# SwiGLU with 22 feature tiles: twenty of them in pairs, and an output projection whose last two tiles come late

## The chip, the cores and the metric

The kernel runs on one core of a Trainium2 chip. The metric is the device time of one execution in microseconds (us); of several runs the median is given. Engines are named as in the profile: PE is TensorE (matmul), PEld its weight load, DVE VectorE, ACT ScalarE, POOL GpSimd, SP SyncE, which issues the DMA transfers here. A line such as L503 is a line of the kernel's source.

## The reference

Four decoder layers, each a token mixer (another kind in each layer) and a SwiGLU channel mixer. Both are wrapped in a modulation by a condition vector and a layer norm. There are 512 tokens of width 1024, all in float32. What matters here is the channel mixer and its frame; its hidden width is 2816.

```python
def swiglu(h, w_in, w_out):
    gu = h @ w_in
    return (jax.nn.silu(gu[..., :FFN_HIDDEN]) * gu[..., FFN_HIDDEN:]) @ w_out

# in reference(), the second half of each layer
h = x * (1 + scale[1][:, None]) + shift[1][:, None]
y = swiglu(h, ffn_w_in[i], ffn_w_out[i])
x = layer_norm(DEEPNORM_ALPHA * x + (1 + gate[1][:, None]) * y.astype(x.dtype), ln_g[i, 1], ln_b[i, 1])
```

## The kernel before

**Tiles.** The hidden width is cut into 22 feature tiles of 128. Everything is held with features on the partitions and the 512 tokens along the free axis. A float32 matmul is made of three matmuls in a reduced type: each operand is split into a high part (a copy on ACT, `wh` for weights) and a low part (a subtraction on DVE, `wl`), and high x high, high x low, low x high are summed (`mm3`, L204 to L206). A weight tile of 128 x 1024 comes by one DMA into a buffer called `raw`, issued by SP.

**A plain tile** needs its gate and its up projection: each 8 steps along the width of 1024, 3 matmuls in each, 512 columns, so 48 matmuls. Then come silu on ACT, the product with the up projection on DVE, and its split in a copy on ACT and a subtraction on DVE (`gated` in `ffn`, L575 to L578), into a tile called `pair`.

**A pair of tiles** is one 2 x 2 block product in Strassen's way (`strassen`): seven products of 24 matmuls of 256 columns instead of eight. They are made in the order 1, 2, 6, 5, 7, 4, 3 of the code. Its weights come as four tiles R0 to R3 by DMA (L495); DVE adds and subtracts some of them (L517, L543), and each product needs one split (L480 on ACT, L481 on DVE). Products 1, 6 and 7 are copied out of their accumulation bank by ACT (L514). The two halves of the tokens are finished apart (gating L555, copy L556, subtraction L557).
The inputs of products 4 to 7 are sums of the input's blocks, made once per layer by `t_forms` (L471 on ACT, L472 on DVE) from four buffers H. These H buffers are taken from the same seven `raw` buffers as the weight tiles, so that four weight tiles can only be loaded once the forms are made.

**The order in a layer.** Tiles 0 and 1 come first (`proj_cols` with "t": all tokens' first half, then the second), then tile 2, then nine pairs (tiles 3 to 20). Tile 21 is a plain tile too; its gate and up projections (`last(0)`, `last(1)`) are placed between products of the last pair. The last two products of each pair are placed among the first products of the next pair.

**Output projection.** It is run in three groups of feature tiles, 7, 8 and 7 (`FGROUPS`), each as soon as its tiles are done: for each of eight blocks of 128 output features one weight tile, 3 matmuls of 512 columns for each feature tile of the group, and an addition into the residual `xz` on DVE (L341). In the last group, blocks 4 to 7 are made in two halves of 256 tokens, so that the layer norm of the first half runs beside the second.
Between the weight splits of the output projections the kernel places loads of conditioning weights (`ada_w`), each followed by a reduction on DVE (L128); `self.rate` says how many per weight tile: 2 in the first two groups, 1 in the last. In layer 3 none is left for the last group.

**What sets the order.** The code above is the order in which work is handed to a scheduler, which puts each engine's instructions in a row; each engine works its row off in that order, and waits where an operand isn't there.

## Time and profile before

| | us |
|---|---|
| median of 3 runs | 2435.06 (2433.79 to 2435.41) |
| the profiled execution | 2436.47 |
| its span in the trace | 2434.8 |
| busy: PE | 2378.1 (98%) |
| busy: DVE | 1794.9 (74%) |
| busy: ACT | 1102.6 (45%) |
| busy: POOL | 481.8 (20%) |

The mean granted clock of TensorE over the span is 0.995 of full speed. The span is what the trace covers of the profiled execution; the 1.7 us beside it lie before and after. Matmuls are pipelined, so the duration of one (0.40 us for 512 columns) is longer than the distance from one start to the next; the distances are what counts in a dense stretch. "Idle before" a group of instructions is time in which that engine waited, and the name behind the arrow is what ended the wait.

### The profile page before, as it was taken

What the parts mean: (1) busy time and instruction counts of PE and PEld (TensorE: products, weight loads), DVE (VectorE), ACT (ScalarE), POOL (GpSimd) and SP (SyncE); (2) the same over time, 40 slices, a digit from 0 to 9 for tenths busy, and PEclk for the clock granted to TensorE, in tenths of its full rate; (3) what the DMA queues carried; (4) which work ended last, traced back from release to release, by engine and by line L of the source; (5) the groups of instructions that cost most, each with busy time, mean ns of one, the idle gap of its engine ahead of it and who ended that gap; (6) DMA issues with size and microseconds to landing.
All of it is one profiled execution on the core that took longest, in us unless ns stands there. A gap on an engine that the chain in (4) does not pass through costs nothing.

```text
span 2434.8 us, 40054 instructions
## 1 busy us (share of the span) xinstructions
PE 2378.1 (98%) x15464; PEld 2123.0 (87%) x15464; DVE 1794.9 (74%) x3137; ACT 1102.6 (45%) x1917; POOL 481.8 (20%) x734
## 2 busy tenths in 40 slices
PE   7999999999899999999999999999999999999998
PEld 5778999998668989899888899898988888999897
DVE  6956988886887978787755569788867556968565
ACT  2534644343553635244333336352445554635343
POOL 5003200004434000006433331000053223100003
PEclk9999999999999999999999999999999999999999
DMA  9832363743411363652521113637525111333331
GB/s 317 285 118 87 105 216 95 245 142 121 144 53 53 103 209 114 232 188 85 162 79 61 35 57 117 205 107 236 186 94 173 62 36 44 109 112 101 106 102 35
DMA packets 93999, 312.31 MB, mean 128 GB/s; under 512 B 10736, under 2 KB 13168, under 8 KB 93808
## 3 DMA queue, kind: packets, MB, share of 16 engines
q1 hardware_dynamic: 92800, 309.43, 39.6%
q8 instruction: 121, 1.98, 0.3%
q14 instruction: 70, 0.57, 0.1%
q10 hardware_dynamic: 1008, 0.32, 0.1%
HBM read 307.62 MB, written 2.10 MB: 127 GB/s over the span
## 4 chain that ended last, share of the span: by engine, by line
PE 80%; DVE 9%; ACT 4%; DMA 3%; POOL 3%; issue 2%; POOLq 0%; ACTq 0%; DVEq 0%; SPq 0%
PE ps L503 27%; PE ps L204 14%; PE ps L206 14%; PE ps L205 14%; DVE wl L195 2%; PE ps L1086 1%; DMA raw<-in_ada_w 1%; PE ps L1252 1%; DVE raw L128 1%; ACT wh L194 1%; PE ps L943 1%; DVE xz L412 1%; POOL H L448 1%; DVE xz L420 1%; DVE hl L449 1%
## 5 line engine op out<-in xcount | busy, mean ns | idle before, releaser
L194 ACT ACTIVATE wh<-raw 128x1024 fp32r<-128x1024 f32 (+1 forms) x251 | 257.9, 1031 | 382.9 <-DMA raw<-in_ffn_out 116.1
L480 ACT ACTIVATE wh<-raw 128x1024 fp32r<-128x1024 f32 x252 | 266.1, 1060 | 351.2 <-PE ps L503 134.2
L503 PE MATMUL ps<-tf,wh 128*128 128x256 f32 x2304 | 410.8, 280 | 0.0
L195 DVE TENSOR_TENSOR wl<-raw,wh 128x1024 fp32r<-128x1024 f32 (+1 forms) x251 | 304.3, 1214 | 99.8 <-ACT wh L194 84.2
L481 DVE TENSOR_TENSOR wl<-raw,wh 128x1024 fp32r<-128x1024 f32 x252 | 305.9, 1221 | 80.1 <-ACT wh L480 78.3
L503 PEld LDWEIGHTS ps<-tf,wh 128*128 128x128 f32 x2304 | 353.3, 188 | 0.9
L503 PE MATMUL ps<-tf,wl 128*128 128x256 f32 x1152 | 321.7, 279 | 0.0
L205 PE MATMUL ps<-pair,wh 128*128 128x512 f32 (+1 forms) x816 | 294.4, 361 | 1.5 <-DVE pair L578 1.3
L204 PE MATMUL ps<-pair,wh 128*128 128x512 f32 (+1 forms) x816 | 294.9, 361 | 0.0
L206 PE MATMUL ps<-pair,wl 128*128 128x512 f32 (+1 forms) x816 | 293.9, 360 | 0.0
L128 DVE CUSTOM_DVE_ANT_0 raw<-raw,cond,adab 128x1024 f32<-128x1024 f32 x192 | 246.6, 1294 | 45.3 <-DMA raw<-in_ada_w 43.9
L341 DVE SCALAR_TENSOR_TENSOR xz<-ps,gate,xz 128x512 f32<-128x512 f32 (+1 forms) x208 | 129.8, 625 | 159.7 <-PE ps L206 159.3
L503 PE MATMUL ps<-hh,wl 128*128 128x256 f32 x864 | 245.0, 284 | 0.0
L503 PE MATMUL ps<-hh,wh 128*128 128x256 f32 x864 | 244.7, 283 | 0.0
L503 PE MATMUL ps<-hl,wh 128*128 128x256 f32 x864 | 244.6, 283 | 0.0
L204 PE MATMUL ps<-wh,hh 128*128 128x512 f32 (+1 forms) x608 | 239.3, 395 | 4.6 <-ACT hh L445 3.3
L204 PE MATMUL ps<-hh,wh 128*128 128x256 f32 (+1 forms) x616 | 208.0, 344 | 18.1 <-ACT wh L194 15.6
L206 PE MATMUL ps<-wh,hl 128*128 128x512 f32 (+1 forms) x608 | 222.5, 366 | 0.0
L205 PE MATMUL ps<-wl,hh 128*128 128x512 f32 (+1 forms) x608 | 222.3, 366 | 0.1
L503 PEld LDWEIGHTS ps<-tf,wl 128*128 128x128 f32 x1152 | 216.7, 188 | 0.0
L206 PE MATMUL ps<-hh,wl 128*128 128x256 f32 (+1 forms) x616 | 209.9, 343 | 5.5 <-DVE wl L195 5.5
L205 PE MATMUL ps<-hl,wh 128*128 128x256 f32 (+1 forms) x616 | 207.9, 340 | 0.2
(292 smaller groups left out, 4957.9 us busy)
## 6 DMA issues: line engine op xcount, KB each, us to landing
raw<-in_ada_w SPq DMA_DIRECT2D x192, 512.0 KB, 4.6
raw<-in_ffn_dp SPq DMA_DIRECT2D x144, 512.0 KB, 3.9
raw<-in_ffn_out SPq DMA_DIRECT2D x64, 448.0 KB, 3.6
raw<-in_ffn_in SPq DMA_DIRECT2D x32, 512.0 KB, 3.7
raw<-in_ffn_out SPq DMA_DIRECT2D x32, 512.0 KB, 4.6
raw<-in_m_vo SPq DMA_DIRECT2D x16, 512.0 KB, 5.8
raw<-in_h_qf SPq DMA_DIRECT2D x16, 512.0 KB, 4.1
raw<-in_h_ig SPq DMA_DIRECT2D x16, 512.0 KB, 3.8
```

The source lines that it names most:

```text
L128: self.nc.vector.tensor_tensor_reduce(w, w, self.cond, 1.0, self.adab[:, sub, j : j + 1], ALU.mult, ALU.add, mod[:, j : j + 1])
L194: nc.scalar.activation(hi[:, :n], raw[:, :n], AF.Copy)
L195: (eng or nc.vector).tensor_tensor(lo[:, :n], raw[:, :n], hi[:, :n].bitcast(F32), ALU.subtract)
L204: nc.tensor.matmul(ps, lhs[0], rhs[0], start=start, stop=False)
L205: nc.tensor.matmul(ps, lhs[0], rhs[1], start=False, stop=False)
L206: nc.tensor.matmul(ps, lhs[1], rhs[0], start=False, stop=stop)
L341: nc.vector.scalar_tensor_tensor(z, ps[:, t], gate[:, d : d + 1], z, ALU.mult, ALU.add)
L412: V.tensor_tensor(z, z, st[:, 0, :], ALU.subtract)
L420: V.tensor_tensor(z, z, st[:, 1, :], ALU.mult)
L480: nc.scalar.activation(hi, raw, AF.Copy)
L481: nc.vector.tensor_tensor(lo, raw, hi.bitcast(F32), ALU.subtract)
L503: nc.tensor.matmul(ps[:, j * 256 : j * 256 + 256], w[a][:, c], m[b], start=first and j == k == a == b == 0, stop=k == 3 and a == 1, skip_g ...
```

## The change

Plain are now only tiles 0 and 1 (`FPLAIN`); tiles 2 to 21 go in ten pairs. The groups are 8, 8 and 6 tiles: tiles 0 and 1 with three pairs, four pairs, three pairs. The function `last` is gone. The last group's output projection gets `late=2`: for its first two blocks it first makes the matmuls of the four tiles of the two earlier pairs, for the one block and the other, and then those of the last pair's two tiles. Only then are the two sums added to the residual; blocks 2 to 7 go as before.

```diff
--- before.py
+++ after.py
@@ constants
 DEPTH = 4
 HID = 2816
 KF = HID // P
-FGROUPS = (7, 8, 7)
-FPLAIN = (0, 1, 2, KF - 1)
+FGROUPS = (8, 8, 6)
+FPLAIN = (0, 1)
 ALPHA = (2 * DEPTH) ** 0.25
 LN_EPS = 1e-5
 RMS_EPS = 1e-6
@@ out_proj
                 done(2 * pair + i, pss[i])
-    def out_proj(self, srcs, per, acts, gate, last):
+    def out_proj(self, srcs, per, acts, gate, last, late=0):
         nc = self.nc
         n = len(acts)
-        def mm(ps, w, o, t):
-            for k in range(n):
+        def mm(ps, w, o, t, ks=range(n)):
+            for k in ks:
                 self.mm3(
                     ps[:, t],
                     [x[:, o + k * P : o + (k + 1) * P] for x in w],
...
             (nc.vector if d == KD - 1 else nc.gpsimd).tensor_tensor(s2, s2, sq, ALU.add)
         halves = (4 * per) if last else 0
-        for d0 in range(0, KD - halves, per):
+        if late:
+            ws = [self.weights(srcs[d], n * P) for d in range(2)]
+            pss = [self.bank() for _ in range(2)]
+            for ks in (range(n - late), range(n - late, n)):
+                for d in range(2):
+                    mm(pss[d], ws[d], 0, slice(0, T), ks)
+                    yield 0.65 * len(ks)
+            for d in range(2):
+                fold(pss[d], d, slice(0, T))
+        for d0 in range(2 if late else 0, KD - halves, per):
             w = self.weights(srcs[d0 // per], per * n * P)
             for i in range(per):
                 ps = self.bank()
@@ ffn
             if i == KD - 2:
                 self.pools("ffn")
                 forms = self.t_forms()
-        pa, pb = self.pair_tile(), self.pair_tile()
+        pa = self.pair_tile()
         yield from first
-        yield from self.proj_cols(src(2), None, lambda ps: gated(pb, 0, *ps))
-        acts = [pa[:, :, 0, :], pa[:, :, 1, :], pb[:, :, 0, :]]
+        acts = [pa[:, :, 0, :], pa[:, :, 1, :]]
         n = (KF - len(FPLAIN)) // 2
         ends = np.cumsum(FGROUPS)
         j0 = 0
-        bank = []
-        def last(x):
-            w = self.weights(src(3)[x], D)
-            ps = self.bank()
-            for k in range(KD):
-                self.mm3(
-                    ps,
-                    [y[:, k * P : (k + 1) * P] for y in w],
-                    [self.hh[:, k, :], self.hl[:, k, :]],
-                    k == 0,
-                    k == KD - 1,
-                )
-            bank.append(ps)
         def begin(i):
             act = self.pair_tile()
...
             nxt = begin(i + 1) if i + 1 < n else None
             if nxt:
                 self.advance(nxt[0], 1)
-            else:
-                last(0)
             self.advance(g, 1)
             if nxt:
                 self.advance(nxt[0], 1)
             self.advance(g, 1)
             yield 0.0
             acts += [act[:, :, 0, :], act[:, :, 1, :]]
-            if nxt is None:
-                last(1)
-                pc = self.pair_tile()
-                gated(pc, 0, *bank)
-                acts.append(pc[:, :, 0, :])
             cur, left = nxt, 5
             gn = len(acts)
             if j0 + gn in ends:
@@ where the last output projection is made
                 for x in self.keep.values():
                     self.nc.gpsimd.memset(x[:, 0, 0:1], 0.0)
-            out = self.out_proj(srcs, per, acts, gate, True)
+            out = self.out_proj(srcs, per, acts, gate, True, 2 if kind == "ffn" else 0)
             while next(out) != "A":
                 pass
             ln = self.layer_norm(subs[i], nxt, 0)
@@ host (layout of the weights)
     r["ffn_in"] = w[..., FPLAIN, :].transpose(0, 4, 2, 3, 1, 5).reshape(DEPTH, len(FPLAIN), P, 2, D)
     n = (KF - len(FPLAIN)) // 2
-    w = w[..., 3 : 3 + 2 * n, :].reshape(DEPTH, 2, 4, P, 2, n, 2, P).transpose(0, 5, 4, 1, 3, 6, 2, 7)
+    w = w[..., 2 : 2 + 2 * n, :].reshape(DEPTH, 2, 4, P, 2, n, 2, P).transpose(0, 5, 4, 1, 3, 6, 2, 7)
     w = w.reshape(DEPTH, n, 4, P, D)
     r["ffn_dp"] = w[:, :, [0, 1, 3, 2]]
     w = f("ffn_w_out").reshape(DEPTH, KF, P, KD, P)
```

The start of the first pair, in layer 0. ACT's row after the input forms, before (`b_390` and `b_391` are the silus of tiles 0 and 1, `wh_2425` the high part of tile 2's up projection, `wh_2487` on those of the pair's weights):

```order
L575 ACT_TABLE_LOAD
L575 ACTIVATE b_390_2407<-ps_2112 128x512
L575 ACTIVATE b_391_2412<-ps_2114 128x512
L194 ACTIVATE wh_2425<-raw_2423 128x1024
L577 ACTIVATE pair_2405<-b_390_2407 128x512
L577 ACTIVATE pair_2405<-b_391_2412 128x512
L575 ACTIVATE b_400_2479<-ps_2429 128x512
L480 ACTIVATE wh_2487<-raw_2485 128x1024
L480 ACTIVATE wh_2520<-raw_2518 128x1024
```

and after (`b_396` is the copy of product 1, `wh_2452` the high part of product 2's weights, `wh_2489` of product 6's):

```order
L585 ACT_TABLE_LOAD
L585 ACTIVATE b_389_2406<-ps_2112 128x512
L585 ACTIVATE b_390_2411<-ps_2114 128x512
L524 ACTIVATE b_396_2448<-ps_2423 128x512
L490 ACTIVATE wh_2452<-raw_2450 128x1024
L587 ACTIVATE pair_2405<-b_389_2406 128x512
L587 ACTIVATE pair_2405<-b_390_2411 128x512
L490 ACTIVATE wh_2489<-raw_2417 128x1024
L490 ACTIVATE wh_2519<-raw_2485 128x1024
```

The copy of product 1 now stands ahead of the split of product 2's weights, and both stand ahead of the copies of tiles 0 and 1; the silu and the copy of tile 2 are gone.

DVE's row at the same place, after the subtractions of the input forms, before (`wl_2426` is the low part for tile 2, `wl_2488` and `wl_2521` those of products 1 and 2 of the pair):

```order
L576 TENSOR_TENSOR b_390_2407<-ps_2113,b_390_2407 128x512
L576 TENSOR_TENSOR b_391_2412<-ps_2115,b_391_2412 128x512
L195 TENSOR_TENSOR wl_2426<-raw_2423,wh_2425 128x1024
L578 TENSOR_TENSOR pair_2405<-b_390_2407,pair_2405 128x512
L578 TENSOR_TENSOR pair_2405<-b_391_2412,pair_2405 128x512
L517 TENSOR_TENSOR raw_2553<-raw_2553,raw_2551 128x1024
L481 TENSOR_TENSOR wl_2488<-raw_2485,wh_2487 128x1024
L481 TENSOR_TENSOR wl_2521<-raw_2518,wh_2520 128x1024
L517 TENSOR_TENSOR raw_2485<-raw_2485,raw_2553 128x1024
L576 TENSOR_TENSOR b_400_2479<-ps_2430,b_400_2479 128x512
```

and after (`raw_2417`, `raw_2450`, `raw_2483`, `raw_2485` are R0 to R3, `wl_2453`, `wl_2490`, `wl_2520` the low parts for products 2, 6 and 5):

```order
L527 TENSOR_TENSOR raw_2485<-raw_2485,raw_2483 128x1024
L586 TENSOR_TENSOR b_389_2406<-ps_2113,b_389_2406 128x512
L586 TENSOR_TENSOR b_390_2411<-ps_2115,b_390_2411 128x512
L491 TENSOR_TENSOR wl_2453<-raw_2450,wh_2452 128x1024
L588 TENSOR_TENSOR pair_2405<-b_389_2406,pair_2405 128x512
L588 TENSOR_TENSOR pair_2405<-b_390_2411,pair_2405 128x512
L527 TENSOR_TENSOR raw_2417<-raw_2417,raw_2485 128x1024
L527 TENSOR_TENSOR raw_2450<-raw_2450,raw_2417 128x1024
L527 TENSOR_TENSOR b_396_2448<-ps_2456,b_396_2448 128x512
L491 TENSOR_TENSOR wl_2490<-raw_2417,wh_2489 128x1024
L491 TENSOR_TENSOR wl_2520<-raw_2485,wh_2519 128x1024
```

The add of R3 and R2 has come to the front of the row. The low part of product 2 stands behind the two products of tiles 0 and 1, and that of product 6 behind the addition of products 1 and 2 (`b_396`). The row of product 1's low part is earlier than what is shown.

The end of the last pair in layer 0. DVE's row before (`b_694` and `b_707` are the two halves of the last pair, `b_727` and `pair_5179` the last plain tile, `wl_5266` and on weights of the output projection):

```order
L555 SCALAR_TENSOR_TENSOR b_694_4855<-ps_4830,b_694_4855 128x512
L195 TENSOR_TENSOR wl_5266<-raw_5263,wh_5265 128x896
L557 TENSOR_TENSOR pair_4823<-b_694_4855,pair_4823 128x2x256
L128 ISA raw_5359,mod_2087<-raw_5359,cond,adab 128x1024
L128 ISA mod_2087 128x1
L517 TENSOR_TENSOR b_707_4989<-ps_4995,b_707_4989 128x512
L195 TENSOR_TENSOR wl_5302<-raw_5299,wh_5301 128x896
L555 SCALAR_TENSOR_TENSOR b_707_4989<-b_713_5049,b_707_4989 128x512
L128 ISA raw_5368,mod_2087<-raw_5368,cond,adab 128x1024
L128 ISA mod_2087 128x1
L557 TENSOR_TENSOR pair_4823<-b_707_4989,pair_4823 128x2x256
L576 TENSOR_TENSOR b_727_5180<-ps_5154,b_727_5180 128x512
```

and after (`b_705` and `b_718` are the two halves of the last pair, `pair_4996`; another reduction L128 stands directly ahead of the first row):

```order
L128 ISA raw_5452,mod_2087<-raw_5452,cond,adab 128x1024
L128 ISA mod_2087 128x1
L565 SCALAR_TENSOR_TENSOR b_705_5028<-ps_5003,b_705_5028 128x512
L195 TENSOR_TENSOR wl_5398<-raw_5395,wh_5397 128x768
L567 TENSOR_TENSOR pair_4996<-b_705_5028,pair_4996 128x2x256
L527 TENSOR_TENSOR b_718_5162<-ps_5168,b_718_5162 128x512
L195 TENSOR_TENSOR wl_5431<-raw_5428,wh_5430 128x768
L565 SCALAR_TENSOR_TENSOR b_718_5162<-b_724_5222,b_718_5162 128x512
L128 ISA raw_5461,mod_2087<-raw_5461,cond,adab 128x1024
L128 ISA mod_2087 128x1
L567 TENSOR_TENSOR pair_4996<-b_718_5162,pair_4996 128x2x256
```

Two reductions of conditioning weights (L128) now stand directly ahead of the first half's gating, and a third ahead of the last subtraction; the gating and the subtraction of the plain tile are gone.

## The prediction

> **What bounds the kernel now.** I read the page's busy shares first, then the chain that ended last, then the PE timeline of the SwiGLU of layer 0 (it begins at 271.94 us), and then ACT, DVE and SP at its two ends, where the change moves work.
>
> ```profile
> PE 2378.1 (98%) x15464; PEld 2123.0 (87%) x15464; DVE 1794.9 (74%) x3137; ACT 1102.6 (45%) x1917; POOL 481.8 (20%) x734
> PE 80%; DVE 9%; ACT 4%; DMA 3%; POOL 3%; issue 2%; POOLq 0%; ACTq 0%; DVEq 0%; SPq 0%
> 374.01 79.84 PE ps L503 x672
> ```
>
> PE is busy 98% of the span and holds 80% of the chain. The third row is one link of it: four pairs, 672 matmuls of 256 columns, without a pause. So two things decide: how many matmul columns PE streams, and whether it must wait. The rates come from the timeline (start, duration, engine, line; in brackets a wait and what ended it).
>
> ```profile
> 271.94 0.40 PE L204 MATMUL ps<-hh,wh 128*128 128x512 f32 x1
> 277.98 0.50 PE L204 MATMUL ps<-hh,wh 128*128 128x512 f32 x1 [0.42 <-ACT wh L194]
> 279.24 0.51 PE L206 MATMUL ps<-hh,wl 128*128 128x512 f32 x1 [0.53 <-DVE wl L195]
> 284.40 0.28 PE L503 MATMUL ps<-hh,wh 128*128 128x256 f32 x1
> ...
> 540.00 0.40 PE L204 MATMUL ps<-hh,wh 128*128 128x512 f32 x1
> 545.48 0.40 PE L503 MATMUL ps<-tf,wh 128*128 128x256 f32 x2
> 551.19 0.40 PE L204 MATMUL ps<-hh,wh 128*128 128x512 f32 x1
> 556.66 0.39 PE L204 MATMUL ps<-pair,wh 128*128 128x512 f32 x1
> 562.08 0.50 PE L205 MATMUL ps<-pair,wh 128*128 128x512 f32 x1 [0.43 <-DVE pair L578]
> ```
>
> The first group is the third plain tile, 48 matmuls between tiles 0 and 1 and the first pair. The second holds the last plain tile: gate (540.00 to 545.48), one product of the last pair, then up (551.19 to 556.66), after which the output projection starts. 24 matmuls of 512 columns take 5.48 us, 0.228 each. A pair takes 79.84 / 4 = 19.96 us, 0.119 per matmul of 256 columns.
>
> **The work on PE.** Per layer, two plain tiles become a pair: four projections at 5.48 us leave (-21.9) and a pair comes (+19.96). In the split halves of the last output projection six tiles stand where seven did, so of the same 22 tiles 24 matmuls of 256 columns (2.87 us) become 12 of 512 in another group (2.73): -0.15. The third tile's block also held its own waits: 284.40 - 271.94 = 12.46 us, of which 48 matmuls explain 10.93; the 1.53 left goes too. Sum: -3.6 us a layer.
>
> **The start of the pairs.** In the old order these 12.46 us of the third tile hide what the first pair needs. In the new order PE runs product 1 of the first pair right after tiles 0 and 1 (from 271.94, 24 x 0.119, to 274.8), and then needs product 2's weights split. The engines at that place:
>
> ```profile
> 270.68 3.90 ACT L471 ACTIVATE tf<-H 128x1024 fp32r<-128x1024 f32 x4 [1.47 <-DVE H L464]
> 274.60 1.28 ACT L575 ACT_TABLE_LOAD   x1
> 275.90 1.09 ACT L575 ACTIVATE b<-ps 128x512 f32<-128x512 f32 x2
> 276.87 1.06 ACT L194 ACTIVATE wh<-raw 128x1024 fp32r<-128x1024 f32 x1
> ...
> 271.77 4.63 DVE L472 TENSOR_TENSOR tf<-H,tf 128x1024 fp32r<-128x1024 f32 x4
> 276.53 1.29 DVE L576 TENSOR_TENSOR b<-ps,b 128x512 f32<-128x512 f32 x2
> 277.96 1.23 DVE L195 TENSOR_TENSOR wl<-raw,wh 128x1024 fp32r<-128x1024 f32 x1
> 279.10 1.29 DVE L578 TENSOR_TENSOR pair<-b,pair 128x512 fp32r<-128x512 f32 x2
> 280.31 1.22 DVE L517 TENSOR_TENSOR raw<-raw,raw 128x1024 f32<-128x1024 f32 x1
> ...
> 273.07 2.55 SPq L495 DMA_DIRECT2D raw<-in_ffn_dp  x3
> DMA to landing us min/median/max: 3.6/3.6/3.6
> L514 ACT ACTIVATE b<-ps 128x512 f32<-128x512 f32 x108 | 62.7, 581 | 7.3 <-PE ps L503 7.3
> ```
>
> ACT first makes the four input forms (to 274.6), then loads the table and does two silus (to 277.0). Behind them now stands the copy of product 1 (0.58, the last row), and only then the split of product 2's weights (1.06): high half at about 278.5. DVE has the forms until 276.4. Then, first in its queue, comes an add of two weight tiles (1.13 by its pitch), which waits for a transfer that can be issued only when a form's buffer is free (273.07) and needs 3.6 to land, 276.7: the add ends at 277.9. Two gated products (1.2 together) end at 279.1, then the low half of product 2's weights (1.2) at 280.3. So PE does two matmuls at 278.5 and the rest of product 2 from 280.35, to 283.0. The third product waits again: DVE has two more subtractions of tiles 0 and 1, two weight adds and the add of product 2 (which waits for PE) ahead of its low half, together 280.3 + 1.2 + 2.3 + 0.6 + 1.2 = 285.6. From there products 6 and 5 run densely, to about 290.9, where four products without a wait end at 283.4. The new wait is +7.5 us a layer. The same order stands at this place in all four layers. After it DVE and ACT catch up: a pair costs DVE about 17 of its 20 us in the stretch of the four pairs below, and the next pair's first split is due 20 us on.
>
> ```profile
> 413.93:433.89 19.96, 19.96 (x171) 19.96 (x170) 17.05 (x19) 11.20 (x15) 0.00 (x0) 1.00 0.36 106
> ```
>
> (Window, PE, weight load, DVE, ACT, POOL busy, clock, DMA.) DVE keeps 2.9 us in hand per pair, and it did not pause while PE waited, so I cost the later pairs at nothing; a debt carried on would only be slower, and is in the upper end.
>
> **The end.** The gate and up projections of the last tile were the cover between the last products of the last pair and the output projection. Now the first two blocks of that projection do their four finished tiles, 24 matmuls, of which six run before the last two products, and 18 x 0.228 = 4.1 us after them. What must happen in these 4.1 us is silu, gating, copy and subtraction of the last half pair: in sum about 3.75 us, with
>
> ```profile
> 542.59 1.28 DVE L128 CUSTOM_DVE_ANT_0 raw<-raw,cond,adab 128x1024 f32<-128x1024 f32 x1 [1.51 <-DMA raw<-in_ada_w]
> 550.64 1.28 DVE L128 CUSTOM_DVE_ANT_0 raw<-raw,cond,adab 128x1024 f32<-128x1024 f32 x1 [2.69 <-DMA raw<-in_ada_w]
> 551.85 0.69 DVE L555 SCALAR_TENSOR_TENSOR b<-ps,b 128x512 f32<-128x512 f32 x1
> 559.14 0.68 DVE L557 TENSOR_TENSOR pair<-b,pair 128x512 fp32r<-128x512 f32 x1
> raw<-in_ada_w SPq DMA_DIRECT2D x192, 512.0 KB, 4.6
> ```
>
> for the price of the DVE steps (ACT's are 0.58 and 0.5). In layer 3's last group no reduction of conditioning weights (L128) stands among them, and the chain fits: 0. In layers 0 to 2 such reductions do stand ahead of the first gating on DVE, and a DVE reduction there waits for its own transfer, 1.51 and 2.69 us in the rows above; one buffer's transfer starts only when the reduction before has freed it and takes 4.6. On the clock of the trace of before the last pair's products end at 547.1 (product 7 ends at 540.05, then six matmuls of the projection and two products), so PE has work until 551.2. The reduction that ends at 542.3 starts the next transfer, which lands at 547, its reduction ends at 548.2, and the first gating (0.6) at 548.8. Behind it stand on DVE two splits of 768 columns (0.9 each, three quarters of 1.22), two subtractions, an add and a gating of 0.6 to 0.7, and one more reduction (1.28): 5.4, so the last subtraction ends at 554.2. PE can do one matmul meanwhile, so it waits about 554.2 - 551.2 - 0.2 = 2.8 us, less the 0.43 of the row at 562.08: +2.4 in each of three layers. From below it is 0 (transfers land earlier than I chain them), from above 4.2 (both waits of the rows above, 1.51 + 2.69). I take 2.4, since the queue's order is certain and only the landing isn't. The layer norm that follows has 1.4 us less of halves to hide in; I cost it at 0, its cover being the halves of the projection, with half a microsecond a layer if the cover is short.
>
> **The clock.** A wait of PE can also lower its granted clock (eighth number of a window).
>
> ```profile
> 1175.47 1.16 PE L1252 MATMUL ps<-b 128*128 128x128 f32 x8 [2.32 <-POOL b L1292]
> 1176.00:1177.00 1.00, 1.00 (x8) 0.96 (x7) 0.34 (x1) 0.00 (x0) 0.84 (x4) 0.86 0.88 311
> 1177.00:1178.00 1.00, 1.00 (x4) 0.72 (x3) 0.70 (x2) 0.25 (x1) 0.92 (x3) 0.50 0.85 320
> 1180.00:1181.00 1.00, 1.00 (x11) 1.00 (x10) 0.47 (x1) 0.00 (x0) 0.43 (x1) 0.94 0.00 0
> 615.23 0.50 PE L204 MATMUL ps<-wh,hh 128*128 128x512 f32 x1 [1.67 <-ACT hh L445]
> 17.03 0.63 PE L206 MATMUL ps<-hh,wl 128*128 128x512 f32 x1
> 17.46 0.63 PE L204 MATMUL ps<-hh,wh 128*128 128x512 f32 x1
> ```
>
> After a wait of 2.32 us the clock is 0.50 from 1176.9 to 1180.2, about 3.4 us; after the wait of 1.67 at 615.23 it isn't. At half clock a 512-column matmul takes 17.46 - 17.03 = 0.43 instead of 0.228, so a spell that falls wholly on matmuls costs 3.4 x (1 - 0.228 / 0.43) = 1.6 us. The new wait (274.8 to 280.35 with two matmuls within) is far longer than 2.32, so I count one spell a layer and take 1.5: +6. From below 0 (the spell falls on the second wait), from above 3 (a second spell after it).
>
> By the Trainium skill, "TensorE: Matmul & The Clock Gate", section "What's actually happening", half clock needs at least one whole idle window of about 3.4 us of a free-running counter. The trace disagrees in part, since 2.32 us were followed by 0.50. By the page a wait of 5.5 us would hold a whole window only about 6 times in 10 (an estimate from its figure), which gives +4 where I take +6.
>
> **The sum.** Per layer -3.6 + 7.5 + 1.5 = 5.4; four layers 21.6; the end adds 3 x 2.4 = 7.2: +29 us. The profiled execution took 2436.47 (span 2434.8), 1.4 above the median of 2435.06; against its own time that gives 2465.3, against the median 2464.
>
> **The rivals.** (A) as above, two waits a layer with a clock spell: +29, own range 2456 to 2472; chance 0.56. For it: the queues are served in order, and the ACT and DVE rows at 274.6 to 280.3 stand ahead of product 2. (B) the waits come, but their spells fall on waiting or don't come: the page's rule too would make it so in part. +23, 2458; the 1.67 row speaks for it, the 2.32 row against; 0.2. (C) two spells in a layer and the end at its upper bound: 15.6 + 12 + 12.6 = +40, 2475; 0.14. (D) the wait at the start is half what I sum, because the transfers land sooner and ACT runs its silus earlier, and the end costs nothing: 4 x (-3.6 + 3.75) = +0.6, 2436. It decides between 2.4 and 4.8 us of wait a layer. Against it: the table load at 274.60 alone takes 1.28 and stands ahead; 0.05. (E) the other side: product 2's weights are split by 274.8, PE never pauses, and the change saves 4 x 3.6 = 14.4: 2421. It decides at a wait of 3.6 us a layer; it needs ACT to do the split ahead of its silus, which the order excludes, or forms made some 5 us earlier, whose rows begin only when DVE has H at 270.68; 0.05. That the late tiles don't hide anything in layers 0 to 2 is no rival but part of the sum: there the 18 matmuls are done before the features are.
>
> **How the numbers follow.** 0.2% (4.9 us) is about what a measurement of this kernel can tell from no change. A, B and C are slower by more: 0.9. D is the same, 0.05, E faster, 0.05. The range of 2449 to 2477 leaves out D and E and little of C; 2449 is B with the end at nothing (+15.6).
>
> **What the profile after would show.** The third tile's row at 277.98 is gone, and a PE row of product 2 (L513 after) near 280 carries a wait for DVE's low half of some 5 us, one of product 6 near 285 a wait of 2 to 3; a window behind them has a clock of 0.50. At the end of layers 0 to 2 a matmul on a pair carries a wait of 2 to 3 us for DVE, in layer 3 none. Four pairs in a row still take 79.84. I am wrong if PE's wait at the start is below 3.6 us a layer, if the scheduler's order hides a product I haven't placed there, or if DVE's debt is carried into each later pair (then even slower).

## The result, and the profile after

The changed kernel takes 2476.33 us (median of 4 runs, 2475.28 to 2478.45), against 2435.2 before (with a fourth run added to the three above): 1.017 times as long, 95% interval 1.0157 to 1.0182. That is +41 us, where +29 was forecast; the time lies at the upper end of the range of 2449 to 2477, in the region of rival C. The profiled execution took 2477.02, its span is 2475.3, 40.5 longer than the span before.

The busy shares of the page after, and one link of its chain of waits (start, duration):

```profile
PE 2386.2 (96%) x15704; PEld 2141.5 (87%) x15704; DVE 1835.2 (74%) x3177; ACT 1122.2 (45%) x1941; POOL 484.8 (20%) x734
396.17 79.84 PE ps L513 x672
```

PE is busy 8.1 us longer in sum (a busy PE at half clock counts too), and the span has grown by 40.5: the rest is waiting. Four pairs in a row still take 79.84.

PE's timeline at the start of the pairs in layer 0, and the rows of ACT and DVE at that place:

```profile
274.63 0.28 PE L513 MATMUL ps<-hh,wl 128*128 128x256 f32 x1
278.42 0.38 PE L513 MATMUL ps<-hh,wh 128*128 128x256 f32 x1 [3.51 <-ACT wh L490]
280.31 0.58 PE L513 MATMUL ps<-hh,wl 128*128 128x256 f32 x1 [1.39 <-DVE wl L491]
287.28 0.39 PE L513 MATMUL ps<-tf,wl 128*128 128x256 f32 x1 [1.25 <-DVE wl L491]
...
276.82 0.60 ACT L524 ACTIVATE b<-ps 128x512 f32<-128x512 f32 x1
277.30 1.07 ACT L490 ACTIVATE wh<-raw 128x1024 fp32r<-128x1024 f32 x1
...
276.69 1.22 DVE L527 TENSOR_TENSOR raw<-raw,raw 128x1024 f32<-128x1024 f32 x1 [0.33 <-DMA raw<-in_ffn_dp]
279.04 1.22 DVE L491 TENSOR_TENSOR wl<-raw,wh 128x1024 fp32r<-128x1024 f32 x1
285.40 0.69 DVE L527 TENSOR_TENSOR b<-ps,b 128x512 f32<-128x512 f32 x1 [1.55 <-PE ps L513]
```

PE has nothing for 3.51 us, does two matmuls, waits for the low half, and waits again before product 6. The add of two weight tiles stands in front on DVE and is itself released by a transfer. The same three waits stand in every layer. The list of groups sums them up (busy, mean ns of one, then idle time ahead and what ended it):

```profile
L513 PE MATMUL ps<-tf,wl 128*128 128x256 f32 x1280 | 356.9, 279 | 5.3 <-DVE wl L491 5.3
L513 PE MATMUL ps<-hh,wl 128*128 128x256 f32 x960 | 276.5, 288 | 5.0 <-DVE wl L491 5.0
L513 PE MATMUL ps<-hh,wh 128*128 128x256 f32 x960 | 276.1, 288 | 14.0 <-ACT wh L490 14.0
```

5.3 + 5.0 + 14.0 = 24.3 us, 6.1 a layer. The clock at that place (window, then PE, PEld, DVE, ACT, POOL busy, clock, DMA share, GB/s):

```profile
280.00:281.00 1.00, 0.69 (x3) 0.69 (x4) 1.00 (x3) 0.00 (x0) 0.00 (x0) 0.50 0.39 160
284.00:285.00 1.00, 1.00 (x7) 1.00 (x7) 0.00 (x0) 0.63 (x1) 0.00 (x0) 0.50 0.00 0
286.00:287.00 1.00, 0.03 (x1) 0.00 (x0) 1.00 (x2) 0.63 (x1) 0.00 (x0) 1.00 0.00 0
```

Product 2 runs at half clock: its 21 last matmuls start 0.21 us apart, against 0.119 at full clock.

The ends, PE's timeline: the waits for the last pair in layers 0 to 2, and those of the layer norms that follow (L395 sums, L412 the norm's transposes; L204 on `wh,hh` is the next mixer's first projection). The waits for the last pair end with ACT's copy, not with DVE's subtraction, which follows it.

```profile
575.30 0.98 PE L204 MATMUL ps<-pair,wh 128*128 128x512 f32 x3 [1.54 <-ACT pair L566]
602.40 0.71 PE L412 MATMUL ps<-ident,lnv 128*128 128x128 f32 x4 [0.70 <-POOL lnv L674]
621.28 0.71 PE L412 MATMUL ps<-ident,lnv 128*128 128x128 f32 x4 [1.12 <-POOL lnv L674]
624.14 0.80 PE L204 MATMUL ps<-wh,hh 128*128 128x512 f32 x1 [2.14 <-ACT hh L455]
1114.77 0.96 PE L204 MATMUL ps<-pair,wh 128*128 128x512 f32 x3 [0.91 <-ACT pair L566]
1142.69 1.87 PE L395 MATMUL ps<-ones,S 128*128 128x1 f32 x8 [5.50 <-DVE S L352]
1801.24 0.96 PE L204 MATMUL ps<-pair,wh 128*128 128x512 f32 x3 [1.45 <-ACT pair L566]
1142.69:1149.00 6.31, 6.30 (x29) 6.31 (x30) 2.80 (x8) 0.98 (x2) 0.72 (x1) 0.50 0.26 77
1850.00:1856.00 6.00, 6.00 (x15) 4.69 (x16) 5.89 (x16) 5.85 (x10) 3.47 (x7) 0.52 0.00 0
```

The 5.50 us at 1142.69, and the half clock after it and after the layer norm of layer 2 (the last two rows), were not in the forecast; a shorter spell of half clock lies behind the layer norm of layer 0, from 623.6 to 627.0. POOL's timeline at the end of layer 1, first the kernel before, then after: the first mask instruction of layer 2's mixer, and the first of the additions into the norm's sums.

```profile
1093.78 0.34 POOL L1160 MEMSET b<- 128x128 f32 x2 [90.44 <-DVE pair L578]
1107.68 1.28 POOL L351 TENSOR_TENSOR S<-S,xz 128x512 f32<-128x512 f32 x1
```

```profile
1115.98 0.34 POOL L1147 MEMSET b<- 128x128 f32 x2 [70.50 <-DVE pair L567]
1130.73 1.30 POOL L352 TENSOR_TENSOR S<-S,xz 128x512 f32<-128x512 f32 x1
```

POOL sits idle for 70 us until the last pair frees the memory that the masks share, then needs 14.7 us until the last of them is made, and the sums of the layer norm stand behind. Before, the sums' first matmul came 27.4 us after that release (1121.15), so the masks were hidden. After, the projection's 24 matmuls on finished tiles lie ahead of the release and the rest is shorter by a tile, so PE asks for the sums at 1137.2, 21.2 us after it.

### The profile page after: what moved, and what is told of

The parts are those of the page before. It is cut to its first block, busy times and chain, and to the rows that moved or that the text cites. A ratio compares the mean times of both kernels' runs of the same rounds, so it can differ in the third digit from the quotient of the medians.

```text
span 2475.3 us, 40608 instructions
## 1 busy us (share of the span) xinstructions
PE 2386.2 (96%) x15704; PEld 2141.5 (87%) x15704; DVE 1835.2 (74%) x3177; ACT 1122.2 (45%) x1941; POOL 484.8 (20%) x734
## 4 chain that ended last, share of the span: by engine, by line
PE 79%; DVE 10%; DMA 3%; POOL 3%; issue 2%; ACT 2%; DVEq 0%; POOLq 0%; ACTq 0%; SPq 0%
PE ps L513 29%; PE ps L204 14%; PE ps L205 13%; PE ps L206 13%; DMA raw<-in_ada_w 2%; DVE raw L128 1%; PE ps L1073 1%; DVE wl L195 1%; PE ps L1239 1%; DVE wl L491 1%; PE ps L930 1%; POOL H L458 1%; ACT wh L194 1%; PE ps L1300 1%; DVE hl L459 1%
## 5 line engine op out<-in xcount | busy, mean ns | idle before, releaser
L513 PE MATMUL ps<-tf,wh 128*128 128x256 f32 x2560 | 457.0, 280 | 0.2 <-ACT b L524 0.2
L491 DVE TENSOR_TENSOR wl<-raw,wh 128x1024 fp32r<-128x1024 f32 x280 | 339.6, 1221 | 77.6 <-ACT wh L490 75.2
L513 PEld LDWEIGHTS ps<-tf,wh 128*128 128x128 f32 x2560 | 392.4, 188 | 2.5 <-ACT b L524 1.8
L513 PE MATMUL ps<-tf,wl 128*128 128x256 f32 x1280 | 356.9, 279 | 5.3 <-DVE wl L491 5.3
L204 PE MATMUL ps<-pair,wh 128*128 128x512 f32 (+1 forms) x800 | 292.1, 366 | 3.9 <-ACT pair L566 3.9
L128 DVE CUSTOM_DVE_ANT_0 raw<-raw,cond,adab 128x1024 f32<-128x1024 f32 x192 | 248.2, 1303 | 64.2 <-DMA raw<-in_ada_w 63.8
L513 PE MATMUL ps<-hh,wh 128*128 128x256 f32 x960 | 276.1, 288 | 14.0 <-ACT wh L490 14.0
L513 PE MATMUL ps<-hh,wl 128*128 128x256 f32 x960 | 276.5, 288 | 5.0 <-DVE wl L491 5.0
L513 PE MATMUL ps<-hl,wh 128*128 128x256 f32 x960 | 275.4, 287 | 0.0
L204 PE MATMUL ps<-wh,hh 128*128 128x512 f32 (+1 forms) x608 | 241.5, 399 | 6.2 <-ACT hh L455 5.0
L513 PEld LDWEIGHTS ps<-hh,wh 128*128 128x128 f32 x960 | 188.0, 196 | 14.8 <-ACT wh L490 14.8
L513 PEld LDWEIGHTS ps<-hh,wl 128*128 128x128 f32 x960 | 187.7, 196 | 6.0 <-DVE wl L491 6.0
L513 PEld LDWEIGHTS ps<-hl,wh 128*128 128x128 f32 x960 | 187.7, 195 | 0.0
```

The costliest lines, as they stand in the source:

```text
L128: self.nc.vector.tensor_tensor_reduce(w, w, self.cond, 1.0, self.adab[:, sub, j : j + 1], ALU.mult, ALU.add, mod[:, j : j + 1])
L204: nc.tensor.matmul(ps, lhs[0], rhs[0], start=start, stop=False)
L491: nc.vector.tensor_tensor(lo, raw, hi.bitcast(F32), ALU.subtract)
L513: nc.tensor.matmul(ps[:, j * 256 : j * 256 + 256], w[a][:, c], m[b], start=first and j == k == a == b == 0, stop=k == 3 and a == 1, skip_g ...
```

## The experiments

The theory after this reading: the loss is made up of the start (waits and half clock) and of the layer end (the short last group takes the cover from the masks and the layer norm), while the saved matmuls are real. In the comparisons "before" is the kernel before, run on the same chip; its median lies between 2434.1 and 2435.2, so a difference of about 1 us between two of the runs below says nothing.

**The start alone.** In the kernel before, tile 2 is moved behind the first pair:

```diff
-        yield from self.proj_cols(src(2), None, lambda ps: gated(pb, 0, *ps))
...
+            if i == 0:
+                yield from self.proj_cols(src(2), None, lambda ps: gated(pb, 0, *ps))
```

> The kernel before with one edit: tile 2 stays a plain tile but is placed behind the first pair, so that the first pair's products follow tiles 0 and 1 directly, as in the change; nine pairs, the last plain tile and the groups 7, 8, 7 stay. Work on PE as before. Theory (the start of the pairs costs what the trace after shows: each layer's first three products end 8.8 to 9.4 us late, of which the old order had 1.5 as waits): +4 x 7.6 = +30, 2466 us, with waits of 3.5, 1.4 and 1.3 us on PE in each layer and half clock behind them. Rival 1 (the waits count, the half clock does not): +4 x (6.2 - 1.5) = +19, 2454. Rival 2 (the debt of the start is made up later, so the loss of the change is elsewhere): within 5 us of 2435.

Measured 2465.71, 1.0129 (1.0112 to 1.0146). The rows of ACT and DVE at the start are the same as in the change, and so are PE's waits:

```profile
278.10 0.39 PE L503 MATMUL ps<-hh,wh 128*128 128x256 f32 x1 [3.50 <-ACT wh L480]
280.05 0.58 PE L503 MATMUL ps<-hh,wl 128*128 128x256 f32 x1 [1.44 <-DVE wl L481]
286.26 0.38 PE L503 MATMUL ps<-tf,wl 128*128 128x256 f32 x1 [1.33 <-DVE wl L481]
```

With PE's work unchanged, the start costs 31.6 us. Rivals 1 and 2 are out.

**The end alone.** The changed kernel with four plain tiles at the start and nine pairs:

```diff
-FPLAIN = (0, 1)
+FPLAIN = (0, 1, 2, 3)
...
```

> The changed kernel with four plain tiles (0 to 3) at the start and nine pairs: the old cover at the start and more, and the new end (groups 8, 8, 6, the last pair's two tiles late, no plain tile at the end). Work on PE as in the kernel before, less 0.15 a layer. Theory: only the losses of the end remain: waits for the last pair of 0.7 to 1.1 more in three layers (+3), the wait of 5.5 us for the layer norm's sums at the end of layer 1 with its half clock (+8), some half clock at the ends of layers 0 and 2 (+3), less the old waits of 1.5 at the start (-6): +8, 2443 us. Rival (the end costs nothing, all of the loss is the start): -6, 2429. Rival 2 (two plain tiles in a row leave DVE less behind, so the end has waits like the old one): 2431 to 2435.

Measured 2452.55 (2448.66 to 2456.79), 1.0075 (1.0059 to 1.009): +18 instead of +8. No wait is left at the start; at the ends PE waits 1.72, 2.30 and 2.51 us for the last pair, 4.77 for the sums in layer 1, and the same 0.70, 1.13 and 2.14 at the norms. Five spells of half clock lie behind these waits. The theory had the right places and too small a price for them.

The two parts alone are more than the change: 31.6 + 18.4, less 8.4 for the pairs in place of plain tiles, plus 6 for the old waits at the start, which both kernels drop and the sum counts twice, is +47.6, not +41. The end is dearer here: the waits for the last pair come to 6.5 us instead of 3.9, and each is followed by half clock, which in the change they are not.

**The masks out of the way.** The masks are built in a tile of their own:

```diff
-            m = self.b2([P, nb, 2, h])
+            m = c.tile([P, nb, 2, h], F32, tag="hm", name=self.nm("hm"))
```

> The changed kernel with one edit: the seven masks of layer 2's mixer are built in a tile of their own instead of a buffer that shares memory with the SwiGLU's, so that POOL can build them long before the end of layer 1. Theory (POOL comes to the layer norm's sums 15 us after the last pair frees its buffer, because 30 mask instructions stand ahead of them in its row): the wait of 5.5 us at the end of layer 1 goes, and the 6.5 us of half clock behind it, together -8 (some 1.6 may come back as another spell of half clock): 2468 us, 2467 to 2471. Rival (the sums wait for the projection itself, the masks only fill POOL's time): 2476.

Measured 2472.76 (2469.23 to 2473.9). The wait of 5.5 us is gone from the trace, and POOL now builds the masks between about 2 and 204 us, in layer 0. The profiled execution is 7.8 us shorter than that of the change, as expected, the median only 3.6, above the 2471 of the theory. In this execution the wait for the last pair in layer 1 was 2.84 instead of 0.91, so a part comes back. So the cause of the wait is shown, its price isn't: the intervals of the two kernels against the one before, 1.014 to 1.017 and 1.0157 to 1.0182, overlap.

**No idle PE at the start.** Sixteen extra matmuls on operands that are there, between products 1 and 2:

```diff
+            bw = self.bank()
+            for x in range(warm):
+                nc.tensor.matmul(bw, w[0][:, :P], self.hh[:, x % KD, :], start=x == 0, stop=x == warm - 1)
...
```

> The changed kernel with 16 additional matmuls of 512 columns in each layer, between products 1 and 2 of the first pair, on operands that are there and into a bank that nobody reads (3.6 us of useless work in the wait of 3.5 us). Theory (the wait is followed by half clock because PE is idle): the low half of product 2's weights still ends at 280.3, but product 2 then runs at full clock, so product 6 starts some 2 us earlier in each layer: -7 to -8, 2469 us, clock 1.00 in the windows from 279 to 285. Rival (the half clock costs nothing, product 6 waits for DVE anyway): 2476. Rival 2 (the extra matmuls delay product 2): 2478 or more.

```profile
279.60 0.39 PE L513 MATMUL ps<-hh,wl 128*128 128x256 f32 x1 [1.21 <-DVE wl L491]
280.00:281.00 1.00, 1.00 (x10) 1.00 (x10) 1.00 (x3) 0.00 (x0) 0.00 (x0) 1.00 0.20 82
```

In the trace the clock stays at 1.00 at all four starts; from the first pair to the first output projection layer 3 takes 78.72 us instead of 80.64, and the profiled execution is 2470.78 instead of 2477.02. So in this execution the half clock at the start is caused by PE's idleness and is worth about 2 us a layer. The median, though, is 2475.29 (2470.78 to 2476.36): as a saving of time over the runs this is inconclusive. The mean granted clock is on record for all four executions: 0.994 in the traced one and 0.991 to 0.993 in the others, against 0.988 to 0.990 in those of the change. So a part of the clock came back in all of them; why the other three are hardly shorter stays open.

**Groups 6, 8, 8.** One constant of the change:

```diff
-FGROUPS = (8, 8, 6)
+FGROUPS = (6, 8, 8)
```

> The changed kernel with the groups 6, 8, 8 instead of 8, 8, 6; nothing else. The last output projection then has eight tiles: six instead of four run before the last pair is needed (36 matmuls instead of 24), and the halves that hide the layer norm are 11.5 us long instead of 8.6. Theory (a third of the loss is the short last group: the layer norm's waits at the ends of all layers with the half clock behind them, and the waits for the last pair): the waits for the last pair and for the norm's sums go, the starts stay: 2476 - 16 = 2460 us, between 2455 and 2464; PE waits only at the starts of the pairs. Rival (the norm's waits come from the order of the rows on POOL and DVE, not from the length of the halves): 2472 to 2477.

Measured 2459.92 (2459.4 to 2460.2), 1.0106 (1.0091 to 1.0122): 16.4 us less than the change. The norm's waits of 0.70 and 1.12 and the 5.50 for the sums are gone, although POOL still builds the masks at the end of layer 1 (1104 to 1117 us); what is left is the start and short waits for the last pair (0.64 in layer 0, 0.83 and 0.64 in layer 1). So the rows alone don't make the wait for the sums, as the rival has it. It takes both: masks ahead of the sums and a last group too short to cover them. Take away either, and the wait is gone.

**Without the late tiles.** `late` is 0, all else is the change:

```diff
-            out = self.out_proj(srcs, per, acts, gate, True, 2 if kind == "ffn" else 0)
+            out = self.out_proj(srcs, per, acts, gate, True, 0)
```

> The changed kernel without the late tiles: the last output projection makes each of its first two blocks in one go (late = 0), groups 8, 8, 6. Theory (the four finished tiles of two blocks are 24 matmuls, 5.5 us, of cover; without them one block's 12 matmuls, 2.7 us, stay, since the first block's finished tiles still come first): the wait for the last pair grows by 2.7 us in each of four layers and brings half clock of some 1 us: +11 to +15 on 2476, 2489 us. Rival (the order of the reductions and of the transfers sets that wait, the late tiles hide nothing): 2476.

Measured 2475.45 (2474.62 to 2476.16), the time of the change: the theory fell. PE's row explains it: in layers 0 to 2 it differs from that of the change in the place of one matmul. With `late` 24 matmuls on finished tiles stand ahead of the first that needs the last pair, without it 22: the scheduler puts them ahead for both blocks without being asked. So nearly all of the cover belongs to the plan of the groups, not to `late`. The waits for the last pair:

```profile
575.06 0.79 PE L204 MATMUL ps<-pair,wh 128*128 128x512 f32 x1 [2.66 <-ACT pair L566]
1115.84 0.50 PE L204 MATMUL ps<-pair,wh 128*128 128x512 f32 x1 [2.70 <-ACT pair L566]
1801.48 0.50 PE L204 MATMUL ps<-pair,wh 128*128 128x512 f32 x1 [2.34 <-ACT pair L566]
```

They are longer than in the change, 7.7 us in sum instead of 3.9. Two matmuls are 0.45 us in each; the rest lies within what these waits differ by among the traces with groups 8, 8, 6 (0.9 to 2.8), and the time shows none of it.

**The gating later, groups 6, 8, 8.** At the start the gating of tiles 0 and 1 is handed over after two products:

```diff
...
+        for j in range(2):
+            gated(pa, j, held[2 * j], held[2 * j + 1])
```

> Groups 6, 8, 8 and, at the start, silu, gating and split of tiles 0 and 1 handed to the scheduler after the first two products of the first pair, so that ACT and DVE split product 2's weights first. Theory (the start waits for what stands ahead in the rows of ACT and DVE): the low half of product 2's weights ends at some 277.6 instead of 280.3 and product 6 starts at 284 instead of 287.3: -3.3 a layer and 0.5 to 1 less of half clock, so 15 us under the run with groups 6, 8, 8 alone: 2445 us. Rival (the start is bound by the transfer into the buffers of H and by the sum of DVE's work, whatever the order): within 4 us of that run.

Measured 2451.06 (2449.09 to 2458.87), 9 us under the groups alone, 15 expected. PE at the start:

```profile
276.99 0.39 PE L513 MATMUL ps<-hh,wl 128*128 128x256 f32 x1 [1.51 <-DVE wl L491]
283.77 0.39 PE L513 MATMUL ps<-tf,wh 128*128 128x256 f32 x1 [1.72 <-ACT wh L490]
```

Product 2's low half now releases PE at 277.0, a little earlier than reckoned, but product 6 waits until 283.8 for ACT's high half. The order counts; it isn't all.

**Four plain tiles, groups 6, 8, 8.**

> Four plain tiles at the start, nine pairs, groups 6, 8, 8, last pair's two tiles late. PE's work as before the change. Theory (24 matmuls of a plain projection for each split of weights cover the start, eight tiles in the last group cover the end): neither the start's waits nor the end's remain, and the old waits of 1.5 and 0.4 a layer go too: 2435 - 6 = 2429 us. Rival (two plain tiles behind each other only move the debt of DVE into the pairs, or the end needs the plain tile): 2436 to 2445.

Measured 2435.83, 1.0005 (0.9996 to 1.0015): the same as before the change, no gain; the theory's 2429 isn't reached, and the lower end of the rival's 2436 to 2446 is met. The start has no wait, but at the end some are there (1.16 and 0.65 for the last pair and 2.12 in the norm of layer 1).

**No reductions beside the last projection.**

```diff
-                    self.rate = 1
+                    self.rate = 0
```

> The changed kernel (groups 8, 8, 6) with no conditioning weights loaded and reduced between the weight tiles of the last group's output projection (rate 0 instead of 1 there); they are all made later, where the kernel makes what is left of them. Theory (the last pair's gating stands on DVE behind reductions that wait for their transfers, so PE waits 0.9 to 2.8 us for the last pair's two tiles at the ends of layers 0 to 2): these waits fall to under 0.5, some 4 to 5 us with the half clock that some of them bring; but eight reductions of 1.3 us move elsewhere in three layers, onto stretches where DVE may be the bound, and cost up to 10. Sum 2465 to 2485; the waits on the last pair decide, not the time. Rival (the wait is the length of the gating's own chain): they stay at 1.5 and more.

Measured 2473.91 (2472.73 to 2474.94). The matmuls on `pair` in the list of groups:

```profile
L204 PE MATMUL ps<-pair,wh 128*128 128x512 f32 (+1 forms) x800 | 292.9, 366 | 0.0
L205 PE MATMUL ps<-pair,wh 128*128 128x512 f32 (+1 forms) x800 | 292.0, 365 | 0.0
```

The waits for the last pair are gone (3.9 and 0.5 us in the change): the reductions and their transfers are their cause; which of the two, this run doesn't tell. The time falls by 2.4 us only.

**A new start, three attempts.** All have ten pairs, groups 6, 8, 8 and later gating; the input forms are made one or two at the old place and the others between the products. The first has one more weight buffer (and two fewer for intermediate results) and the other forms' subtractions on POOL, the second those on POOL without that buffer, the third the buffer and all forms on DVE. The first two also have the masks in a tile of their own, the third hasn't, and the third hands the gating over one product later; so they differ in more than POOL. The third's edit, cut:

```diff
-        self.raw = pool("raw", 7)
+        self.raw = pool("raw", 8)
...
-        for i, r in ((6, b22), (5, b11), (7, b12), (4, b21)):
+        for n, (i, r) in enumerate(((6, b22), (5, b11), (7, b12), (4, b21))):
+            if n in (1, 2):
+                yield forms
...
```

> Ten pairs, groups 6, 8, 8, late tiles, the masks of layer 2 in a tile of their own, and a new order at the start: one more buffer for weight tiles (8; 5 instead of 7 for intermediate results), so that all four weight tiles of the first pair can be loaded before the input forms are made; only the form of product 6 is made at the old place, the other three after product 2's weights, with their subtractions on POOL; the gating of tiles 0 and 1 comes after the first three products. Theory (the start's 9 us a layer are DVE's and ACT's row, not a law of the pairs): the low half of product 2's weights ends at 276.4, of product 6's at 278.7; waits of 1.5 us a layer are left, below what brings half clock; 2460 - 4 x 7.7 = 2429 us. Rival (five buffers for intermediate results, or POOL's slower subtractions, make new waits in the pairs): 2436 to 2450.

> As the run with the new order at the start, but with seven buffers for weight tiles (and seven for intermediate results) as in the change, and two forms at the old place instead of one. Theory (of the start's wait some 3.5 us are the transfer of the fourth weight tile into a buffer that a form must free, 3.6 us after its issue): one wait of 2 to 3.5 us before product 6 stays in each layer, with half clock behind some: 2438 to 2446 us. Rival (the order of the rows is all that matters, the transfer isn't on the path): 2429 as the other run.

Measured 2462.89 (2459.2 to 2464.35) and 2463.97 (2461.27 to 2468.23): the first misses its theory by 34 us, the second by 18 us, and both lie above their rivals' times too. DVE and POOL in the first (the last row is the first of POOL's three instructions alone):

```profile
274.71 1.22 DVE L493 TENSOR_TENSOR wl<-raw,wh 128x1024 fp32r<-128x1024 f32 x1
275.97 3.32 DVE L529 TENSOR_TENSOR raw<-raw,raw 128x1024 f32<-128x1024 f32 x1
279.21 6.68 DVE L493 TENSOR_TENSOR wl<-raw,wh 128x1024 fp32r<-128x1024 f32 x2
286.41 1.21 DVE L555 TENSOR_TENSOR raw<-raw,raw 128x1024 f32<-128x1024 f32 x1
273.82 10.98 POOL L484 TENSOR_TENSOR tf<-H,tf 128x1024 fp32r<-128x1024 f32 x3 [6.29 <-ACT tf L483]
273.82 4.39 POOL L484 TENSOR_TENSOR tf<-H,tf 128x1024 fp32r<-128x1024 f32 x1 [6.29 <-ACT tf L483]
```

POOL subtracts from 273.8 to 284.8. DVE's instruction at 274.71 still takes 1.22, while POOL's first takes 4.39; from 276.0 on the two engines take turns, and DVE's next three take 3.3 us each instead of 1.2. PE waits 3.50 for product 6's low half. In the second run two adds of weight tiles at 276.8 take 5.2 us together beside POOL, ACT's split waits for the later one, and PE waits 4.82 for it in each layer. So with the help by POOL the start was as slow as it had been.

> Ten pairs, groups 6, 8, 8, eight buffers for weight tiles, and the new order at the start with all input forms on DVE: the form of product 6 at the old place, that of product 5 after product 6's weights, the last two after product 5, then the gating of tiles 0 and 1. The masks stay where the change has them. Theory (the run with POOL's subtractions failed at the start because DVE's instructions took 3.3 us instead of 1.2 while POOL worked; the order itself is right): DVE's instructions take 1.2 us again, product 2 runs from 275.9, product 6 right behind it, waits of 1 to 2.5 us a layer are left and little half clock: 2460 - 4 x 6.5 to 7.5 = 2430 to 2434 us, the kernel before or slightly better. Rival (five buffers for intermediate results, or the sum of DVE's work, bind at the next products): 2440 to 2452.

PE's waits at the start of layer 0, a window there, and a wait in layer 1's mixer:

```profile
274.98 0.38 PE L515 MATMUL ps<-tf,wh 128*128 128x256 f32 x1 [0.63 <-ACT wh L492]
285.10 0.38 PE L515 MATMUL ps<-tf,wl 128*128 128x256 f32 x1 [0.76 <-DVE wl L493]
276.00:284.00 8.00, 7.94 (x67) 7.73 (x66) 8.00 (x10) 6.07 (x9) 0.00 (x0) 1.00 0.60 189
648.68 0.48 PE L990 MATMUL ps<-ident,b 128*128 128x128 f32 x1 [4.17 <-POOL b L874]
```

Measured 2439.18 (2435.67 to 2441.41), 1.0016 (1.0007 to 1.0025). The start's waits are down to 1.4 us in a layer with the clock at 1.00: 21 of the 25 us that the groups had left are back, which shows that they came from the order of the rows and the missing buffer together; the share of each is open. The theory's 2430 to 2434 is missed by 5, and no kernel here beats the one before. DVE is busy all 8 us of that window, and a wait of 4.17 for POOL in layer 1's mixer (1.60 before) has taken a part of what was won.

## Why the prediction was right, point by point

The direction and the two places that were priced, the start of the pairs and the wait for the last pair, came out as forecast. That the time lies within 2449 to 2477, 0.7 us below the upper end, is partly luck: rival A, which had the best chance, gave 2456 to 2472 as its own range and missed. A term put at nothing cost some 15 us, and another that was priced 4 us too high made up for a part of it. The steps in turn:

**The work on PE** (-3.6 a layer, -14.4 in sum): right. A pair takes 79.84 / 4, and the third tile's waits are gone with it. Layer 3, where nothing waits for the last pair, shows it: from the first matmul of its SwiGLU (2071.66 before, 2105.51 after) to the end of the span it is 6.6 us longer, and 9.3 for the start, less 3.6, plus 0.6 at the last norm is 6.3 (the 9.3 is worked out in the next paragraph).

**The start** (7.5 of waits and 1.5 of clock, 9.0 a layer): right in its place and its cause; its size came out by two errors that cancel, which is luck. The chain along ACT and DVE was as reckoned to a tenth of a microsecond (high half 278.4, low half 280.3). Layer 3 after, from the first product to the first output projection, and the same point in layer 0 before, where the first product starts at 284.40:

```profile
2128.40 0.28 PE L513 MATMUL ps<-hh,wh 128*128 128x256 f32 x1
2209.04 0.40 PE L204 MATMUL ps<-pair,wh 128*128 128x512 f32 x1
335.73 0.40 PE L204 MATMUL ps<-pair,wh 128*128 128x512 f32 x1
```

Layer 3 takes 80.64 us for 600 matmuls, which at the 51.33 for 432 of the trace before would be 71.3: 9.3 in this layer. The other three, taken the same way, lose 9.3, 9.2 and 8.6, so all four lose 36.4. But the waits are 6.1, not 7.5, and the clock makes up the rest, 3.2 in layer 3, not 1.5. The spell is two of the old spells long (6.8 us, from 278.8 to 285.7), and because product 2 runs more slowly, less of DVE's chain is left to wait for. Rival B, no loss by the clock, is excluded by the windows; rivals D and E by the waits of 24.3 us in sum.

The prediction took the price of half clock from two matmuls at 17.03 and 17.46, where the profile gives no clock below 1.00, so those rows don't show what they are used for. In the trace after, matmuls of 512 columns in a window at 0.50 are 0.43 apart too, so the price itself holds:

```profile
1853.13 0.63 PE L205 MATMUL ps<-wl,hh 128*128 128x512 f32 x1
1853.56 0.63 PE L204 MATMUL ps<-wh,hh 128*128 128x512 f32 x1
1853.00:1854.00 1.00, 1.00 (x4) 0.71 (x4) 1.00 (x3) 1.00 (x3) 0.23 (x2) 0.50 0.00 0
```

By the Trainium skill, "TensorE: Matmul & The Clock Gate", section "What's actually happening", a wait of 3.51 us would hold a whole idle window of 3.41 only rarely (an estimate: 3 times in 100). In the trace all four starts were followed by half clock, and so was the wait of 2.14 at 624.14; the trace and the page disagree, and the sum went rightly by the trace.

**The end** (2.4 in each of three layers): right in cause, too large in size. The waits are 1.71, 1.09 and 1.63 us with their second parts, less 0.43 each: +3.1 instead of 7.2. The sum leaned on a reduction that ends at 542.3, which no row shows (in the trace before two of them end at 539.9 and 543.9). In the traces of kernels with groups 8, 8, 6 that keep the reductions these waits are 0.9 to 2.8, inside the range from 0 to 4.2; that they differ because the transfers land at different times is likely, but not shown. And the prediction credited `late` with the cover of 18 matmuls; the run without it shows that the scheduler gives nearly all of that cover anyway.

**The layer norm** (cost at 0, with half a microsecond a layer if the cover is short): this is the term that was mis-sized. The step said "its cover being the halves of the projection" and reckoned only that they are 1.4 us shorter. What else hangs on the last pair wasn't asked: POOL's masks begin when it is done, and the sums stand behind them. The waits (5.50 in layer 1; 0.70, 1.12 and 0.5 more than before in layers 0 and 2; 0.6 in layer 3) come to 10.7 us, and half clock comes with them in layers 0 to 2. In the other direction the wait of 2.32 us at 1175.47 in layer 2's mixer, with its half clock, has shrunk to 0.59 without any. As the rest of 40.5 the term is 40.5 - (36.4 - 14.4 + 3.1) = 15.4 us; less the 4.1 by which the end was priced too high, this makes up nearly all of the 12 us between forecast and measurement. The groups 6, 8, 8, which give the cover back, take 16.4 off, the end's waits in part among them.

Rival C had the right sum for another reason: its second spells of clock came, its price at the end did not.

## What to carry to other kernels

Count the cover in matmuls per split of weights: a plain projection gives PE 5.48 us for each pair of ACT and DVE instructions, a product of a pair 2.87, so the cheaper arithmetic feeds on the engines that were hiding the start. When tiles move to a later end, list everything in every engine's row that is released by the last of them (here masks on POOL, with the norm's sums behind) and measure from that release to the first PE instruction that needs it. And try the longest group last: the constant that cost 16 us here, 8, 8, 6 against 6, 8, 8, did no work of its own. It is one comparison; other orders were not run.

## What the runs showed of the hardware

DVE's subtraction of two SBUF operands of 128x1024 took 3.3 us beside POOL's of the same kind, when POOL's had begun first, and 1.2 without it. The Trainium skill, "SBUF — State Buffer", section "Terms", has DVE and GpSimd share a pair of ports that one instruction holds to its end; the rows agree (1.2 of its own and some 2.1 of waiting), and they show the size: an engine that was idle made the loaded one nearly three times as slow.

Half clock came with PE's waits of 3.5 us in each of the four layers, and lasted 6.8 us each time in the change; in the run of the start alone two of its four spells lasted 3.4 and two 6.8. It isn't decided by one wait's length alone: in the run with the later gating it came in layer 0 right after a wait of 1.51 (from 277.3) and again after one of 1.72 (from 284.1), while one of 1.67 in the kernel before was not followed by it. Sixteen useless matmuls in the wait kept the clock at 1.00 in the one traced execution.
